# Matmul operands and weight loads: where the buffers start modulo 512 bytes

## The chip, the cores and the metric

One core of a Trainium2 chip runs the whole kernel as one program. The metric is the device time of that program in microseconds, the median of several runs. All buffers that are spoken of here lie in the on-chip memory (SBUF), which has 128 partitions; a buffer starts at the same byte in each of them. TensorE runs each matmul as two instructions: a weight load, which puts the stationary operand (128x128 numbers, 512 bytes in each partition) into the array, and the matmul, which streams the moving operand (256 or 512 numbers, 1024 or 2048 bytes in each partition) through it. The profile shows them as PEld and PE.

## The reference

The reference is one layer of a decoder trunk for 256 tokens of width 2048, all in float32: adaLN modulation from a condition vector, four token mixers on one input projection, an output projection, and a gated feed-forward net of width 5632.

```python
mod = (silu(c) @ w_mod + b_mod)              # sh1, sc1, g1, sh2, sc2, g2
h = rmsnorm(x, norm_mix) * (1 + sc1) + sh1
proj = h @ w_in                              # 2048 x 5660, for all four mixers
y = concat([gla(...), gated_deltanet(...), pool(...), forgetting_attention(...)]) @ w_out
x = x + g1 * y
h = rmsnorm(x, norm_ffn) * (1 + sc2) + sh2
gate = causal_dwconv(h @ w_gate, conv_w) + conv_b
x = x + g2 * ((silu(gate) * (h @ w_up)) @ w_down)
out = rmsnorm(x, norm_final)
```

## The kernel before

Every large product is made of three matmuls on numbers that are split in two: a high part (a cast to float32r, by ScalarE) and a low part (the difference, by VectorE). `split` (L113 to L116) does it; its two instructions are the groups L115 ACT CAST and L100 DVE TENSOR_TENSOR. The product is high x high + high x low + low x high.

Weights are streamed in blocks of 128x1024 numbers. `load` (L155) brings one into `wr` (five buffers, in turn), `load_split` makes `wh` and `wl` of it (three buffers each, in turn). The activations stand in one large buffer, `bigA`: high and low parts of the normalised input (`HL`), then of the mixers' outputs (`Y2`), then of the second normalised input (`H2`), each 2048 bytes to a block `k` of 128 features: 256 tokens of high part, 256 of low part. All matmuls go through the helper `mm` (L97), so that the profile tells them apart by their tiles alone: out<-moving,stationary.

The stages in order of time:

- Input projection (`ext` and `acc` as outputs, from about 60 to 478 us, in the second half between the mixers' own small products `gdt`, `oxt` and the condition's products `bgt`). `gdn` and `pair` run, for each block and each 128 outputs, three matmuls of 256 columns: `wh` as stationary with the high and the low activations moving, then `wl` with the high ones. Some pairs (`tok`) have it the other way round: activations stationary, `wh`, `wl`, `wh` moving.
- Output projection (`project`, `wot`, to 547 us): activations stationary, `wh`, `wl`, `wh` moving; 512 columns wide, in the last two of five chunks 256.
- Feed-forward, gate and up (`proj`, outputs `fpt` from `bigA`, about 553 to 1046 us): 22 calls of `proj` with 16 blocks `k` each. For a block: four weight loads of `wh`, each with one matmul of 512 columns (the high and the low activations side by side), and four of `wl`, each with one matmul of 256 columns (the high ones). This document calls such a block, eight matmuls, a step; there are 352.
- Feed-forward, down (`fpt` from `AH`, `AL`, 1046 to 1289 us): stationary is `AH` (high part of the gated activations) twice, then `AL` (low part); moving is `wh`, `wl`, `wh`, always 512 wide. 1056 matmuls.

The weight load of the next matmul runs while a matmul runs. So while a matmul of gate and up reads `bigA`, the load reads `wh` or `wl`; while one of down reads `wh` or `wl`, the load reads `AH` or `AL`. The document names such a pair by its distance: start of what the load reads minus start of what the matmul reads, modulo 512 bytes. All blocks within a buffer are multiples of 512 bytes, so that one number holds for a whole buffer.

Where the buffers lie follows from the order and the size of the tiles in the pools `keep` (first) and `wp` (second), then the pools of the phases. In the built program:

| buffer | start, before | mod 512 | start, after | mod 512 |
|---|---|---|---|---|
| `bigA` | 19808 | 352 | 19360 | 416 |
| `wr` (first) | 73120 | 416 | 72608 | 416 |
| `wh` (first) | 93600 | 416 | 93088 | 416 |
| `wl` (first) | 105888 | 416 | 105440 | 480 |
| `AH` | 134560 | 416 | 134560 | 416 |
| `AL` | 179616 | 416 | 179680 | 480 |

Of the kernel before, what the change touches and what calls it, by code (L numbers as in the profile page):

```python
# [8 lines left out]
F32 = mybir.dt.float32  # L9
F32R = mybir.dt.float32r  # L10
# [6 lines left out]
P = 128  # L17
D = 2048
KT = D // P
T = 256  # L20
NT = T // P
FF = 5632
NF = FF // P
# [23 lines left out]
NG = len(GROUPS)  # L47

TAKE = (16, 12, 11)

ORDER = "gpfd"

# [21 lines left out]
def trunk_kernel(ctx: ExitStack, tc: tile.TileContext, x, c, w_mod, b_mod, norm_mix, norm_ffn, w_in,  # L74
# [3 lines left out]
    nc = tc.nc  # L78
# [12 lines left out]
    wp = ctx.enter_context(tc.tile_pool(name="wp", bufs=3))  # L91

    def kt_(shape, name, dt=F32):
        return keep.tile(shape, dt, name=name, tag=name)

    def mm(o, l, r, start=True, stop=True):
        PE.matmul(o, lhsT=l, rhs=r, start=start, stop=stop, skip_group_check=True)  # L97

    def tt(o, a, b, op):
        V.tensor_tensor(out=o, in0=a, in1=b, op=op)  # L100
# [13 lines left out]
    def split(hi, lo, src):  # L114
        S_.copy(hi, src)  # L115
        tt(lo, src, hi.bitcast(F32), ALU.subtract)  # L116
# [4 lines left out]

    ident = kt_([P, P], "ident")
    nc.sync.dma_start(ident, cst[:, K_ID:K_ID + P])
    crow = kt_([KT, P], "crow")
    nc.sync.dma_start(crow, c[0].rearrange("(k p) -> k p", p=P))
    ones = kt_([P, P], "ones")
    V.memset(ones, 1.0)

# [12 lines left out]
    s2 = kt_([P, KT], "s2")  # L141
    sh2 = kt_([P, KT], "sh2")

    bigA = lambda: keep.tile([P, KT, 2 * T], F32R, name="bigA", tag="bigA")
    bigC = lambda: keep.tile([P, KT * T], F32, name="bigC", tag="bigC")

# [6 lines left out]
    def load(view, k0, nk, c0, n):  # L153
        wr = wp.tile([P, 1024], F32, name="wr", tag="wr", bufs=5).rearrange("p (k n) -> p k n", n=n)
        nc.sync.dma_start(wr[:, 0:nk], view[:, k0:k0 + nk, c0:c0 + n])  # L155
        return wr

    def load_split(view, k0, nk, c0, n):
        wr = load(view, k0, nk, c0, n)
        wh = wp.tile([P, 1024], F32R, name="wh", tag="wh", bufs=3).rearrange("p (k n) -> p k n", n=n)  # L160
        wl = wp.tile([P, 1024], F32R, name="wl", tag="wl", bufs=3).rearrange("p (k n) -> p k n", n=n)
        split(wh[:, 0:nk], wl[:, 0:nk], wr[:, 0:nk])
        return wh, wl

# [63 lines left out]
    with ExitStack() as ph:  # L228
# [59 lines left out]
        with ExitStack() as st:  # L288
            sp = st.enter_context(tc.tile_pool(name="sp", bufs=1, reuse_waits="tile"))
            acp = st.enter_context(tc.tile_pool(name="acp", bufs=1, space=PSUM, reuse_waits="tile"))  # L290
            xt = sp.tile([P, NT, D], F32, name="xt")
            r1 = sp.tile([P, P], F32, name="r1")
            r2 = sp.tile([54, P], F32, name="r2")
            r3 = sp.tile([2 * NF, P], F32, name="r3")
# [115 lines left out]
            def gdn(g):  # L410
                k0, nk = GROUPS[g]
                for k2 in range(k0, k0 + nk, 2):
                    for c3 in range(3):
                        wh, wl = load_split(wi_v, k2, 2, C_QKV + 512 * c3, 512)
                        for kk in range(2):
                            k = k2 + kk
                            for f in range(4):
                                ft = c3 * 4 + f
                                o = acc[ft // 2][:, ft % 2]
                                fs = slice(f * P, f * P + P)  # L420
                                mm(o, wh[:, kk, fs], HL[:, k, 0:T], start=False, stop=False)
                                mm(o, wh[:, kk, fs], HL[:, k, T:], start=False, stop=False)
                                mm(o, wl[:, kk, fs], HL[:, k, 0:T], start=False, stop=k == KT - 1)
                        yield
# [13 lines left out]
            def pair(p, g0, g1):  # L438
                c0, tok, dst, scale = pairs[p]
                k0, k1 = GROUPS[g0][0], sum(GROUPS[g1 - 1])  # L440
                a = ext().rearrange("p (f t) -> p f t", t=T)
                for ka in range(k0, k1, 4):
                    kb = min(ka + 4, k1)
                    wh, wl = load_split(wi_v, ka, kb - ka, c0, 256)
                    for f in range(2):
                        for k in range(ka, kb):
                            fs = slice(f * P, f * P + P)
                            first, last = f == 0 and k == k0, k == k1 - 1
                            if tok:
                                xh, xl = HL[:, k, fs], HL[:, k, T + f * P:T + f * P + P]  # L450
                                three = ((xh, wh[:, k - ka]), (xh, wl[:, k - ka]), (xl, wh[:, k - ka]))
                            else:
                                xh, xl = HL[:, k, 0:T], HL[:, k, T:]
                                three = ((wh[:, k - ka, fs], xh), (wh[:, k - ka, fs], xl), (wl[:, k - ka, fs], xh))
                            for i, (l, r_) in enumerate(three):
                                mm(a[:, f], l, r_, start=first and i == 0, stop=last and i == 2)
                    yield
                with tc.high_priority():
                    add(dst, a, g0 == 0, scale)
# [10 lines left out]
            def extras(g):  # L470
                ps = range(len(pairs) - TAKE[g], len(pairs)) if g < NG - 1 else range(len(pairs))
                for p in ps:
                    yield from pair(p, done[p], g + 1)
                    done[p] = g + 1
# [472 lines left out]
        chunks = ((0, 512), (512, 512), (1024, 512), (1536, 256), (1792, 256))  # L947
        Y2 = bigA()

        def project(n, a):  # L950
            c0, w = chunks[n]
            nk = 1024 // w
            for j in range(KT // nk):
                ks = order[nk * j:nk * j + nk]
                if n == 0:
                    for k in ks:
                        split(Y2[:, k, 0:T], Y2[:, k, T:], pr[:, k + 4])
                wh, wl = load_split(wo_v, ks[0], nk, c0, w)
                steps = [(kk, k, t) for kk, k in enumerate(ks) for t in range(NT)]
                if n == len(chunks) - 1 and ks[-1] == order[-1]:  # L960

                    steps.sort(key=lambda s: s[2])
                for kk, k, t in steps:
                    st, sp_ = j + kk == 0, nk * j + kk == KT - 1
                    xh, xl = Y2[:, k, t * P:t * P + P], Y2[:, k, T + t * P:T + t * P + P]
                    mm(a[t], xh, wh[:, kk], start=st, stop=False)
                    mm(a[t], xh, wl[:, kk], start=False, stop=False)
                    mm(a[t], xl, wh[:, kk], start=False, stop=sp_)
# [5 lines left out]
        x1 = bigC().rearrange("p (t d) -> p t d", t=NT)  # L974
        for t in range(NT):
            nc.sync.dma_start(x1[:, t], x_v[:, t])
        x1s = kt_([P, NT, len(chunks)], "x1s")
        with tc.tile_pool(name="op", bufs=2, reuse_waits="tile") as op:
            for n, (c0, w) in enumerate(chunks):
                ns, gs = slice(c0, c0 + w), slice(c0 % 1024, c0 % 1024 + w)  # L980
# [11 lines left out]
    with ExitStack() as ph:  # L992
# [27 lines left out]
                stt(H2[:, k, T:], h, sh2[:, k:k + 1], H2[:, k, 0:T].bitcast(F32), ALU.add, ALU.subtract)  # L1020

        ap_ = ph.enter_context(tc.tile_pool(name="ap", bufs=1, reuse_waits="tile"))
        AH = ap_.tile([P, NF, T], F32R, name="AH")
        AL = ap_.tile([P, NF, T], F32R, name="AL")

        def proj(gp, view, c0):
# [17 lines left out]
        with tc.tile_pool(name="gp", bufs=2, reuse_waits="tile") as gp:  # L1044
            for n in range(NF // 4):
                gt = proj(gp, wg_v, 512 * n)
                ut = proj(gp, wu_v, 512 * n)
                for i in range(4):
                    f = 4 * n + i
# [6 lines left out]
                    tt(cv, ut[i], cv, ALU.mult)  # L1056
                    split(AH[:, f], AL[:, f], cv)

# [3 lines left out]
        with tc.tile_pool(name="op2", bufs=1, reuse_waits="tile") as op:  # L1062
            chunks = ((0, 512), (512, 512), (1024, 512), (1536, 512))
            fs = op.tile([P, NT, len(chunks) + 1], F32, name="fs")
            f1 = op.tile([P, 4], F32, name="f1")
            for n, (c0, w) in enumerate(chunks):
# [6 lines left out]
                for g in range(NF // nk):  # L1073
                    wh, wl = load_split(wd_v, nk * g, nk, c0, w)
# [5 lines left out]
                    for k, t, h_, l_ in steps:  # L1080
                        ts = slice(t * P, t * P + P)
                        mm(a[t], AH[:, k, ts], h_, start=k == 0, stop=False)
                        mm(a[t], AH[:, k, ts], l_, start=False, stop=False)
                        mm(a[t], AL[:, k, ts], h_, start=False, stop=k == NF - 1)
# [58 lines left out]
```

## Time and profile before

| | us |
|---|---|
| median of three runs | 1299.4 |
| lowest, highest | 1298.0, 1302.43 |
| the profiled execution | 1305.52 |
| its span, first to last instruction | 1303.7 |
| TensorE busy in the span | 1247.2 (96%) |
| VectorE, ScalarE busy | 888.9 (68%), 636.6 (49%) |
| mean granted TensorE clock | 0.981 |

The rows of a group read: line, engine, operation, out<-moving,stationary, shape, count, then busy time in us, mean duration of one in ns, and the engine's idle time before them. The end of a matmul is modelled and matmuls overlap, so that a duration is longer than the step from one start to the next; a matmul's own slowness shows in both.

### The profile page before, as it was taken

Reading aid. Unit: us, or ns where it says so; the run is one execution under the profiler, and the core shown is the slowest. Engines: PE = TensorE matmul, PEld = TensorE weight load, DVE = VectorE, ACT = ScalarE, POOL = GpSimd, SP = SyncE. Lnnn points to the kernel's source line nnn. Section 1 sums busy time; section 2 is a strip of 40 time slices with the busy share of each in tenths; the row PEclk is TensorE's granted clock in tenths of the full one; section 3 lists DMA queues with packets and bytes.
Section 4 is the critical chain, followed back from the end, with each engine's and each line's share of the span. In section 5 each row is a group of like instructions: output and inputs, shape, how many; then the busy total and the mean of one; then the engine's idle time right before and its main releaser. Section 6 shows DMA issues by size and latency. Waiting matters only on the chain.

```text
span 1303.7 us, 19845 instructions
## 1 busy us (share of the span) xinstructions
PE 1247.2 (96%) x7663; PEld 1078.8 (83%) x7663; DVE 888.9 (68%) x1201; ACT 636.6 (49%) x1000; POOL 23.5 (2%) x31
## 2 busy tenths in 40 slices
PE   2799999999999999999999999999999999999995
PEld 1699999898976687888888888888888888888884
DVE  7578797989763387676666656665756687974543
ACT  3455344674364454555555545554555553443432
POOL 0200000010000000000000000000000000000000
PEclk8799999999999999999999999999999999999998
DMA  9999998796557888656666666657666699875662
GB/s 329 270 367 377 320 335 295 250 336 224 174 200 255 311 315 286 176 148 190 180 196 192 180 197 190 190 165 211 190 184 175 208 353 381 306 258 188 194 193 82
DMA packets 168597, 311.91 MB, mean 239 GB/s; under 512 B 16172, under 2 KB 54067, under 8 KB 167863
## 3 DMA queue, kind: packets, MB, share of 16 engines
q1 hardware_dynamic: 168503, 310.65, 72.9%
q8 instruction: 60, 0.98, 0.3%
q14 instruction: 34, 0.28, 0.1%
HBM read 308.51 MB, written 2.10 MB: 238 GB/s over the span
## 4 chain that ended last, share of the span: by engine, by line
PE 91%; DMA 4%; DVE 1%; SPq 1%; ACT 1%; issue 1%; POOLq 0%; ACTq 0%; DVEq 0%
PE fpt L97 56%; PE ext L97 16%; PE wot L97 5%; PE gdt L97 4%; PE acc L97 4%; DMA wm<-in_w_mod_dram 4%; PE bgt L97 3%; PE oxt L97 2%; DMA wr<-in_w_in_dram 1%; DVE ga L103 1%; ACT xT L1011 0%; DVE m L100 0%; DVE wl L100 0%; SPq L399 0%; PE oxt L873 0%
## 5 line engine op out<-in xcount | busy, mean ns | idle before, releaser
L100 DVE TENSOR_TENSOR wl<-wr,wh 128x1024 fp32r<-128x1024 f32 x384 | 469.0, 1222 | 296.8 <-ACT wh L115 296.1
L115 ACT CAST wh<-wr 128x1024 fp32r<-128x1024 f32 x384 | 403.5, 1051 | 490.2 <-PE fpt L97 314.9
L97 PE MATMUL fpt<-bigA,wh 128*128 128x512 f32 x1408 | 399.3, 395 | 2.1 <-DVE bigA L103 2.1
L97 PEld LDWEIGHTS fpt<-bigA,wh 128*128 128x128 f32 x1408 | 239.0, 188 | 32.8 <-issue 2.2
L97 PEld LDWEIGHTS fpt<-bigA,wl 128*128 128x128 f32 x1408 | 222.8, 189 | 34.5 <-DVE wl L100 3.7
L97 PE MATMUL fpt<-bigA,wl 128*128 128x256 f32 x1408 | 240.7, 279 | 0.0
L103 DVE SCALAR_TENSOR_TENSOR ga<-wm,cond,ga 128x1024 f32<-128x1024 f32 x139 | 177.9, 1280 | 14.1 <-DMA wm<-in_w_mod_dram 13.2
L97 PE MATMUL ext<-bigA,wh 128*128 128x256 f32 x768 | 138.4, 282 | 0.0
L97 PE MATMUL fpt<-wl,AH 128*128 128x512 f32 x352 | 137.5, 391 | 0.0
L97 PE MATMUL fpt<-wh,AL 128*128 128x512 f32 x352 | 137.0, 389 | 0.0
L97 PE MATMUL fpt<-wh,AH 128*128 128x512 f32 x352 | 123.4, 390 | 0.0
L97 PEld LDWEIGHTS ext<-bigA,wh 128*128 128x128 f32 x768 | 118.5, 190 | 3.1 <-DVE E L100 0.8
L97 PE MATMUL ext<-bigA,wl 128*128 128x256 f32 x384 | 107.9, 281 | 1.7 <-DVE wl L100 1.7
L97 PEld LDWEIGHTS fpt<-wl,AH 128*128 128x128 f32 x352 | 66.1, 188 | 14.3 <-DVE wl L100 0.4
L97 PEld LDWEIGHTS fpt<-wh,AH 128*128 128x128 f32 x352 | 66.1, 188 | 14.1 <-ACT wh L115 0.2
L97 PEld LDWEIGHTS fpt<-wh,AL 128*128 128x128 f32 x352 | 66.1, 188 | 14.0 <-issue 0.2
L97 PEld LDWEIGHTS ext<-bigA,wl 128*128 128x128 f32 x384 | 72.9, 190 | 2.9 <-DVE wl L100 1.9
L97 PE MATMUL acc<-bigA,wh 128*128 128x256 f32 x384 | 68.7, 285 | 5.6 <-ACT bigA L115 3.2
L97 PE MATMUL ext<-wh,bigA 128*128 128x256 f32 (+1 forms) x320 | 69.3, 308 | 0.0
L97 PEld LDWEIGHTS acc<-bigA,wh 128*128 128x128 f32 x384 | 59.7, 195 | 6.0 <-ACT bigA L115 3.3
L97 PE MATMUL wot<-wh,bigA 128*128 128x512 f32 (+1 forms) x256 | 63.0, 337 | 0.0
L97 PEld LDWEIGHTS ext<-wh,bigA 128*128 128x128 f32 x320 | 52.9, 192 | 5.5 <-issue 1.4
(340 smaller groups left out, 1193.2 us busy)
## 6 DMA issues: line engine op xcount, KB each, us to landing
wm<-in_w_mod_dram SPq DMA_DIRECT2D x192, 512.0 KB, 5.6
wr<-in_w_in_dram SPq DMA_DIRECT2D x88, 512.0 KB, 9.1
wr<-in_ffn_w_gate_dram SPq DMA_DIRECT2D x88, 512.0 KB, 3.7
wr<-in_ffn_w_up_dram SPq DMA_DIRECT2D x88, 512.0 KB, 4.3
wr<-in_ffn_w_down_dram SPq DMA_DIRECT2D x88, 512.0 KB, 4.6
wr<-in_w_out_dram SPq DMA_DIRECT2D x32, 512.0 KB, 4.2
xt<-in_x_dram SPq DMA_DIRECT2D x2, 1024.0 KB, 7.1
bigC<-in_x_dram SPq DMA_DIRECT2D x2, 1024.0 KB, 9.1
```

The lines of the kernel that those rows point to most:

```text
L97: PE.matmul(o, lhsT=l, rhs=r, start=start, stop=stop, skip_group_check=True)
L100: V.tensor_tensor(out=o, in0=a, in1=b, op=op)
L103: V.scalar_tensor_tensor(out=o, in0=a, scalar=s, in1=b, op0=op0, op1=op1)
L115: S_.copy(hi, src)
```

## The change

Three things move the buffers. `x1s` (a small tile of sums) and `crow` (the condition vector as rows) change pools, so that `bigA` starts 64 bytes later modulo 512. The three buffers of `wh` become three tiles of their own, and the third is 64 bytes longer, so that `wl` starts 64 bytes beyond `wh` modulo 512. In the feed-forward phase a filler tile ahead of `AH` and 64 bytes behind it put `AH` at the same place as `bigA` and `wh`, and `AL` 64 bytes beyond.

```diff
+LINE = 64
...
-    crow = kt_([KT, P], "crow")
-    nc.sync.dma_start(crow, c[0].rearrange("(k p) -> k p", p=P))
...
+    x1s = kt_([P, NT, 5], "x1s")
...
+    loads, whs = [0], []
+
     def load_split(view, k0, nk, c0, n):
         wr = load(view, k0, nk, c0, n)
-        wh = wp.tile([P, 1024], F32R, name="wh", tag="wh", bufs=3).rearrange("p (k n) -> p k n", n=n)
+        i = loads[0] % 3
+        loads[0] += 1
+        if loads[0] == 1:
+            for j in range(3):
+                whs.append(wp.tile([P, 1024], F32R, name=f"wh{j}", tag=f"wh{j}", bufs=1,
+                                   padded_shape=[P, 1024 + LINE // 4 * (j // 2)]))
+            wh = whs[0]
+        else:
+            wh = wp.tile([P, 1024], F32R, name=f"wh{i}", tag=f"wh{i}", bufs=1) if loads[0] > 3 else whs[i]
         wl = wp.tile([P, 1024], F32R, name="wl", tag="wl", bufs=3).rearrange("p (k n) -> p k n", n=n)
+        wh = wh.rearrange("p (k n) -> p k n", n=n)
...
+            crow = sp.tile([KT, P], F32, name="crow")
+            nc.sync.dma_start(crow, c[0].rearrange("(k p) -> k p", p=P))
...
-        x1s = kt_([P, NT, len(chunks)], "x1s")
...
-        AH = ap_.tile([P, NF, T], F32R, name="AH")
+        ap_.tile([P, (512 - LINE) // 4], F32, name="gap")
+        AH = ap_.tile([P, NF * T], F32R, name="AH", padded_shape=[P, NF * T + LINE // 4]).rearrange("p (f t) -> p f t", t=T)
```

The built program has the same instructions in the same order on every engine and queue as before, but for one separate wait of ScalarE ahead of the first copy into `AH`, which is gone. What changes otherwise is addresses alone. The distances, by stage:

| stage, matmul running -> next load | distance before | after |
|---|---|---|
| gate/up, 512 wide -> `wh` (three of four) | 64 | 0 |
| gate/up, 512 wide -> `wl` (the fourth) | 64 | 64 |
| gate/up, 256 wide -> `wl` (three of four) | 64 | 64 |
| gate/up, 256 wide -> `wh` (the fourth) | 64 | 0 |
| down, all | 0 | 0 |
| `gdn`, `pair`: next load `wh` (two of three) | 64 | 0 |
| `gdn`, `pair`: next load `wl` (one of three) | 64 | 64 |
| `project`, `tok`: `wh` moving (two of three) | 448 | 0 |
| `project`, `tok`: `wl` moving (one of three) | 448 | 448 |

## The prediction

> **What bounds the kernel now.** I read the page first, its busy times and its chain that ended last, to see which engine a change must shorten.
>
> ```profile
> PE 1247.2 (96%) x7663; PEld 1078.8 (83%) x7663; DVE 888.9 (68%) x1201; ACT 636.6 (49%) x1000; POOL 23.5 (2%) x31
> ...
> PE 91%; DMA 4%; DVE 1%; SPq 1%; ACT 1%; issue 1%; POOLq 0%; ACTq 0%; DVEq 0%
> ```
>
> TensorE holds 91% of the chain. The chain in order of time has one piece that covers the whole feed-forward net, with no other engine in it:
>
> ```profile
> 553.49 734.96 PE fpt L97 x3875
> ```
>
> So 735 us, more than half of the span, end when the matmuls end, and a nanosecond on each of them comes out at the end. The view by stretches says how full the two halves are (columns: length, PE, PEld, DVE, ACT, POOL busy, granted clock, DMA share, GB/s):
>
> ```profile
> 553.50:1046.10 492.60, 492.60 (x2816) 427.55 (x2817) 311.89 (x452) 261.41 (x399) 0.00 (x0) 1.00 0.63 186
> 1046.20:1289.00 242.80, 242.80 (x1065) 199.24 (x1064) 159.11 (x154) 100.53 (x114) 0.95 (x1) 1.00 0.71 251
> ```
>
> Clock 1.00 in both, VectorE at 312 of 493 us, DMA at 0.63: nothing but the matmuls' own pace. That pace is the thing to look at, and two views give it. First the groups, shapes kept apart, gate/up in the first two rows, down in the other three:
>
> ```profile
> L97 PE MATMUL fpt<-bigA,wh 128*128 128x512 f32 x1408 | 399.3, 395 | 2.1 <-DVE bigA L103 2.1
> L97 PE MATMUL fpt<-bigA,wl 128*128 128x256 f32 x1408 | 240.7, 279 | 0.0
> L97 PE MATMUL fpt<-wl,AH 128*128 128x512 f32 x352 | 137.5, 391 | 0.0
> L97 PE MATMUL fpt<-wh,AL 128*128 128x512 f32 x352 | 137.0, 389 | 0.0
> L97 PE MATMUL fpt<-wh,AH 128*128 128x512 f32 x352 | 123.4, 390 | 0.0
> ```
>
> The same instruction, 128x512 with a 128x128 weight load beside it, lasts 395 ns on average in gate/up (distance 64) and 389 to 391 in down (distance 0). Then the order of time, ten steps of gate/up and ten matmuls of down; the first column is the start:
>
> ```profile
> 700.25 1.09 PE L97 MATMUL fpt<-bigA,wh 128*128 128x512 f32 x4
> 701.17 0.62 PE L97 MATMUL fpt<-bigA,wl 128*128 128x256 f32 x4
> ...
> 714.11 1.09 PE L97 MATMUL fpt<-bigA,wh 128*128 128x512 f32 x4
> 715.04 0.62 PE L97 MATMUL fpt<-bigA,wl 128*128 128x256 f32 x4
> ```
>
> ```profile
> 1150.05 0.39 PE L97 MATMUL fpt<-wh,AL 128*128 128x512 f32 x1
> ...
> 1152.31 0.39 PE L97 MATMUL fpt<-wh,AL 128*128 128x512 f32 x1
> ```
>
> Ten steps take 714.11 - 700.25 = 13.86 us, 1386 ns each. In down ten matmuls start between the two rows (nine rows, the first of the two among them, and one of the nine holds two) in 2.26 us, 226 ns each. At down's pace four matmuls of 512 take 904 ns; in gate/up they take 920 to 930.
>
> Where in the step the excess sits is seen by asking for stretches so short that one matmul alone runs in them. The four of 512 in one step (from 802.06 us), in order, then the four of 256, two at a time:
>
> ```profile
> L97 PE MATMUL fpt<-bigA,wh 128*128 128x512 f32 x1 | 0.4, 388 | 0.0
> L97 PE MATMUL fpt<-bigA,wh 128*128 128x512 f32 x1 | 0.4, 398 | 0.0
> L97 PE MATMUL fpt<-bigA,wh 128*128 128x512 f32 x1 | 0.4, 393 | 0.0
> L97 PE MATMUL fpt<-bigA,wh 128*128 128x512 f32 x1 | 0.4, 398 | 0.0
> L97 PE MATMUL fpt<-bigA,wl 128*128 128x256 f32 x2 | 0.4, 278 | 0.0
> L97 PE MATMUL fpt<-bigA,wl 128*128 128x256 f32 x2 | 0.4, 276 | 0.0
> ```
>
> The excess comes in pieces of 5 ns: none, two, one, two; then one on the first of 256 (a mean of 278 for two), none on the rest. Something is lost in whole pieces while a matmul and a load read at once at distance 64, and in down, at distance 0, hardly anything.
>
> **The change, part by part.** It issues the same instructions in the same order. What costs or gains is what each pair of readers does at its new distance.
>
> *Gate/up, the first three matmuls of 512 of each step: 64 to 0.* Nearest row: down, the same shapes at distance 0. 388 + 398 + 393 = 1179 ns become three of 389 or 390: 9 to 12 ns a step, times 352 steps = 3.2 to 4.2 us. All on the path. I take 3.8.
>
> *Gate/up, the fourth of 512 (the next load is `wl`): stays at 64.* It lasts 398 now. It may stay (0), or, following three undisturbed ones, behave like the first of a step now does (388): 10 ns x 352 = 3.5 us. I take 0.5, near the lower end, since its own distance is not changed and its row says 398.
>
> *Gate/up, 256 wide.* The first has one piece (5 ns, 1.8 us over 352), the others next to none; the group's mean of 279 against 276 for an undisturbed one bounds it all: 3 ns x 1408 = 4.2 us. The first follows the fourth of 512, whose fate it probably shares; the last gets distance 0. No row shows 256 wide at distance 0, so a loss stands open too, bounded by one piece on that last one: 5 x 352 = 1.8 us. I take a gain of 0.5 between -1.8 and +4.2.
>
> *Down: 0 before, 0 after,* since `AL` moves along with `wl` and `AH` stays with `wh`. Nothing, both ways.
>
> *Input projection, 256 wide.* One undisturbed stretch, the four main groups:
>
> ```profile
> L97 PE MATMUL ext<-bigA,wh 128*128 128x256 f32 x160 | 27.7, 278 | 0.0
> L97 PE MATMUL acc<-bigA,wh 128*128 128x256 f32 x138 | 23.3, 278 | 0.0
> L97 PE MATMUL ext<-bigA,wl 128*128 128x256 f32 x80 | 22.3, 278 | 1.7 <-DVE wl L100 1.7
> L97 PE MATMUL acc<-bigA,wl 128*128 128x256 f32 x67 | 17.5, 278 | 0.0
> ```
>
> Their counts in the whole run (the means here hold waits too):
>
> ```profile
> L97 PE MATMUL ext<-bigA,wh 128*128 128x256 f32 x768 | 138.4, 282 | 0.0
> L97 PE MATMUL ext<-bigA,wl 128*128 128x256 f32 x384 | 107.9, 281 | 1.7 <-DVE wl L100 1.7
> L97 PE MATMUL acc<-bigA,wh 128*128 128x256 f32 x384 | 68.7, 285 | 5.6 <-ACT bigA L115 3.2 <-ACT wh L115 2.4
> L97 PE MATMUL acc<-bigA,wl 128*128 128x256 f32 x192 | 52.2, 284 | 0.8 <-DVE wl L100 0.8
> ```
>
> 2 ns above 276, on 768 + 384 + 384 + 192 = 1728 matmuls: 3.5 us if every pair became clean; two of three go to distance 0: 2.3 us. The other bound is a loss: a piece of 5 ns instead of 2 on those two thirds, 1152 x 3 = 3.5 us. Not all would reach the end, since before 257 us a wait for weights ends on DMA, not on TensorE:
>
> ```profile
> 249.34 7.75 DMA wm<-in_w_mod_dram
> ```
>
> What is won ahead of it is waited away there as long as that transfer does not come sooner. I take 1.0.
>
> *Output projection.*
>
> ```profile
> L97 PE MATMUL wot<-wh,bigA 128*128 128x512 f32 x128 | 40.4, 394 | 0.0
> L97 PE MATMUL wot<-wh,bigA 128*128 128x256 f32 x128 | 22.8, 279 | 0.0
> ```
>
> 394 against 390 on `wh` at 448, of which there are 128 and in the first chunk 64 more: 192 x 4 = 0.8 us; 279 against 276: 128 x 3 = 0.4 us. The pairs that stay at 448 gain nothing. I take 0.8 of 0 to 1.2 (the products before 257 us that have activations as weights are within the rounding of this).
>
> *`crow`, `x1s`, filler, the lost wait.* `crow`'s transfer is at the same place in SP's queue. `split` now writes `wl` 64 bytes off from `wr` and `wh`; should VectorE slow down by it, its 312 busy us in the 492.6 of gate/up leave room for half as much again. ScalarE's lost wait stood once, beside TensorE's work. Nothing.
>
> *Sum.* 3.8 + 0.5 + 0.5 + 1.0 + 0.8 = 6.6 us off. The profiled execution took 1305.5 (span 1303.7 and 1.8 around it) and would take 1298.9; it is 6.1 above the median of the three runs, which lies in no step of the sum, so I take it off the median: 1299.4 - 6.6 = 1292.8.
>
> **A rule that speaks against it.** The Trainium skill, "TensorE: Matmul & The Clock Gate", Part 2 (Step-by-step), says that TensorE has two independent read ports and that loading the next weights takes no read bandwidth from the running matmul; "SBUF — State Buffer" (Who interferes with whom) adds "PE and ACT never wait on anyone". By this rule no address changes a pace, and the sum would be 0. The rows above stand against it, 388 to 398 ns for one instruction at full clock with nothing else different in the step, but they do not prove that addresses are the cause.
>
> **The rivals.**
>
> 1. *Distance is not the cause; the time stays.* What is lost may come of alternating widths (512, then 256) or of PSUM, since gate/up has both widths and down one. For it: within one step at one and the same distance the loss is 0, 10, 5, 10. Against it: `wot` at 512 alone, no widths alternating, has 394 at distance 448, where down has 390. Time: 1299.4. This is also what the rule of the skill gives.
>
> 2. *In line is worse where widths alternate; slower.* At distance 0 both readers start at the same place modulo 512 at nearly the same time. If in gate/up each of 512 then lost two pieces (398) and each of 256 one (281, that is 278 x 2 - 276 = 280 by the row), it would cost 1408 x (398 - 394) + 1408 x (280 - 277) = 5.6 + 4.2 = 9.8 us: 1309. It decides from 1.4 ns per matmul on (3.9 us over 2816). Against it: down's 1056 matmuls at distance 0, at 389 to 391, show no piece.
>
> 3. *All of the loss goes, also where the distance stays 64.* If the pieces are handed on from one matmul to the next (the first of a step is clean at 64), one clean matmul makes the next clean. Then a step takes 4 x 226 + 4 x 113 = 1356 to 1360 ns instead of 1386: 26 to 30 ns x 352 = 9 to 10.5 us, with 3 us from the projections some 13: 1286.5. For it: the history in the step. Against: the fourth of 512 has its own distance.
>
> **How the numbers follow.** A measurement of this kernel tells about 0.3%, 3.9 us, from no change. The forecast (4 to 10 us off, 1289.5 to 1295.5) has 0.58; rival 3 (beyond 10 us) 0.10; rival 1, or gains too small to tell, 0.22; rival 2 or any loss beyond 0.3% 0.10. So faster 0.68, same 0.22, slower 0.10. The range runs from rival 3's time, 1286.5, to just above no change, 1300, and leaves out rival 2 and the tails. Predicted: 1292.8.
>
> **What would show it.** In the profile after: `fpt<-bigA,wh` at 391 to 393 on average instead of 395; in one step 389, 389, 389 and then, in question, 398 or 388 on the fourth; ten steps in 13.70 to 13.75 us (13.6 by rival 3); down unchanged at 389 to 391 and 226 ns a matmul; the piece of chain `fpt` some 5 us shorter than 734.96; `wot` at 512 near 391. The prediction is wrong if the step still takes 1386 ns (rival 1), if the three in line show 393 or 398 (rival 2), or if gate/up gains and the projections lose as much because 256 wide at distance 0 is worse than at 64.

## The result and the profile after

The changed kernel takes 1311.78 us (median of 4 runs, 1310.86 to 1313.0) against 1299.62 for the kernel before beside it: ratio 1.0085, 95% interval [1.0071, 1.01], some 11 us slower by the ratio, 12 by the medians. The forecast was 1292.8, faster than before.

The page after, groups with shapes kept apart, the same five as before (a helper's line is now L99 instead of L97):

```profile
L99 PE MATMUL fpt<-bigA,wh 128*128 128x512 f32 x1408 | 398.8, 395 | 2.1 <-DVE bigA L105 2.1
L99 PE MATMUL fpt<-bigA,wl 128*128 128x256 f32 x1408 | 244.6, 282 | 0.0
L99 PE MATMUL fpt<-wl,AH 128*128 128x512 f32 x352 | 138.4, 393 | 0.0
L99 PE MATMUL fpt<-wh,AL 128*128 128x512 f32 x352 | 138.2, 392 | 0.0
L99 PE MATMUL fpt<-wh,AH 128*128 128x512 f32 x352 | 125.1, 395 | 0.0
```

The first row is what was to go from 395 to 392: it stands still. The second went from 279 to 282. And down, whose own distances were 0 and stayed 0, went from 391, 389 and 390 to 393, 392 and 395. The chain's piece of the feed-forward net says the same in one number, 742.24 for 734.96 us:

```profile
553.11 742.24 PE fpt L99 x3875
```

It is split by stretches. The first stretch is gate/up, 3.6 us longer than the 492.6 of before, at the same full clock and with the same number of matmuls; the rest of the 7.3 us is down:

```profile
553.20:1049.40 496.20, 496.20 (x2816) 432.73 (x2817) 311.86 (x452) 261.58 (x399) 0.00 (x0) 1.00 0.62 185
```

In order of time, ten steps of gate/up, and ten matmuls of down:

```profile
700.83 1.09 PE L99 MATMUL fpt<-bigA,wh 128*128 128x512 f32 x4
701.75 0.64 PE L99 MATMUL fpt<-bigA,wl 128*128 128x256 f32 x4
...
714.83 1.09 PE L99 MATMUL fpt<-bigA,wh 128*128 128x512 f32 x4
715.75 0.52 PE L99 MATMUL fpt<-bigA,wl 128*128 128x256 f32 x3
```

```profile
1160.19 0.40 PE L99 MATMUL fpt<-wh,AL 128*128 128x512 f32 x1
...
1162.50 0.39 PE L99 MATMUL fpt<-wh,AL 128*128 128x512 f32 x1
```

A step takes 14.00 us / 10 = 1400 ns (1386 before): 920 ns for the four of 512, as before, and 480 for the four of 256, about 15 more. Down takes 231 ns a matmul (226 before). The four of 512 in one step, each from a stretch that holds it alone:

```profile
L99 PE MATMUL fpt<-bigA,wh 128*128 128x512 f32 x1 | 0.4, 396 | 0.0
L99 PE MATMUL fpt<-bigA,wh 128*128 128x512 f32 x1 | 0.4, 397 | 0.0
L99 PE MATMUL fpt<-bigA,wh 128*128 128x512 f32 x1 | 0.4, 389 | 0.0
L99 PE MATMUL fpt<-bigA,wh 128*128 128x512 f32 x1 | 0.4, 392 | 0.0
```

So distance 0 does not give 389 at once: the first two of a step, just after four of 256, are slow, the third is clean. In the input projection (the same stretch as before, 120 to 180 us) 278 has become 282:

```profile
L99 PE MATMUL ext<-bigA,wh 128*128 128x256 f32 x160 | 28.5, 282 | 0.0
L99 PE MATMUL ext<-bigA,wl 128*128 128x256 f32 x80 | 22.7, 283 | 1.7 <-DVE wl L102 1.7
L99 PE MATMUL acc<-bigA,wh 128*128 128x256 f32 x129 | 22.3, 282 | 0.0
```

4 ns on the 1728 matmuls of that kind would be 7 us. From start to start, over the whole input projection, the two traces have 114.9 and 117.9 ns on average for such a matmul where none waits, which makes about 5 us. The single profile of before does not show them in its total, since it happened to reach the output projection late: its first `wot` piece starts at 478.34 us, that of the changed kernel at 477.41, those of later kernels with the old places in the input projection between 471.63 and 477.21.

### The profile page after: what moved, and what is told of

It reads as the page before. It is cut to its first block, busy times and chain, and to the rows that moved or that the text cites. A ratio compares the mean times of both kernels' runs of the same rounds, so it can differ in the third digit from the quotient of the medians.

```text
span 1310.6 us, 19844 instructions
## 1 busy us (share of the span) xinstructions
PE 1257.0 (96%) x7663; PEld 1086.6 (83%) x7663; DVE 889.4 (68%) x1201; ACT 635.7 (49%) x1000; POOL 22.7 (2%) x31
## 4 chain that ended last, share of the span: by engine, by line
PE 91%; DMA 5%; DVE 1%; SPq 1%; ACT 1%; issue 1%; POOLq 0%; ACTq 0%; DVEq 0%
PE fpt L99 57%; PE ext L99 16%; PE wot L99 5%; PE gdt L99 4%; PE bgt L99 3%; PE acc L99 3%; DMA wm<-in_w_mod_dram 3%; PE oxt L99 2%; DMA wr<-in_w_in_dram 1%; DVE ga L105 1%; DMA ct<-in_cst_dram 0%; ACT xT L1024 0%; ACT wh L117 0%; DVE wl L102 0%; DVE m L102 0%
## 5 line engine op out<-in xcount | busy, mean ns | idle before, releaser
L117 ACT CAST wh<-wr 128x1024 fp32r<-128x1024 f32 x384 | 403.1, 1050 | 497.6 <-PE fpt L99 320.7
L99 PE MATMUL fpt<-bigA,wh 128*128 128x512 f32 x1408 | 398.8, 395 | 2.1 <-DVE bigA L105 2.1
L99 PEld LDWEIGHTS fpt<-bigA,wh 128*128 128x128 f32 x1408 | 242.4, 190 | 33.2 <-issue 2.2
L99 PEld LDWEIGHTS fpt<-bigA,wl 128*128 128x128 f32 x1408 | 223.9, 188 | 32.5 <-DVE wl L102 4.0
L99 PE MATMUL fpt<-bigA,wl 128*128 128x256 f32 x1408 | 244.6, 282 | 0.0
L99 PE MATMUL ext<-bigA,wh 128*128 128x256 f32 x768 | 139.9, 283 | 0.0
L99 PE MATMUL fpt<-wl,AH 128*128 128x512 f32 x352 | 138.4, 393 | 0.0
L99 PE MATMUL fpt<-wh,AL 128*128 128x512 f32 x352 | 138.2, 392 | 0.0
L99 PE MATMUL fpt<-wh,AH 128*128 128x512 f32 x352 | 125.1, 395 | 0.0
L99 PEld LDWEIGHTS ext<-bigA,wh 128*128 128x128 f32 x768 | 118.0, 188 | 3.0 <-issue 1.2
L99 PE MATMUL ext<-bigA,wl 128*128 128x256 f32 x384 | 108.6, 283 | 1.7 <-DVE wl L102 1.7
L99 PEld LDWEIGHTS fpt<-wl,AH 128*128 128x128 f32 x352 | 66.1, 188 | 15.4 <-DVE m L102 0.2
L99 PEld LDWEIGHTS fpt<-wh,AL 128*128 128x128 f32 x352 | 66.1, 188 | 15.4 <-issue 0.2
L99 PEld LDWEIGHTS fpt<-wh,AH 128*128 128x128 f32 x352 | 66.2, 188 | 15.0 <-ACT wh L117 0.2
L99 PEld LDWEIGHTS ext<-bigA,wl 128*128 128x128 f32 x384 | 73.5, 192 | 2.8 <-DVE wl L102 1.9
L99 PE MATMUL acc<-bigA,wh 128*128 128x256 f32 x384 | 70.7, 289 | 3.7 <-ACT bigA L117 2.6
L99 PE MATMUL ext<-wh,bigA 128*128 128x256 f32 (+1 forms) x320 | 69.9, 310 | 0.0
L99 PEld LDWEIGHTS acc<-bigA,wh 128*128 128x128 f32 x384 | 60.3, 196 | 4.1 <-ACT bigA L117 2.7
L99 PE MATMUL wot<-wh,bigA 128*128 128x512 f32 (+1 forms) x256 | 63.4, 338 | 0.0
L99 PEld LDWEIGHTS ext<-wh,bigA 128*128 128x128 f32 x320 | 53.1, 193 | 5.7 <-issue 1.4
```

## The experiments

Three accounts of the loss: *distance* (as forecast: a pair at 0 is clean, anything else pays), *mixture* (loads and matmuls that follow each other at different places modulo 512 disturb each other), *place* (480 itself is bad). Each kernel is timed against the kernel before on the same chip. The diffs are shortened; "..." and words in brackets stand for code.

### All in line, at three places, and AL alone

```diff
# all416: the kernel before, x1s ahead of bigA
+    x1s = kt_([P, NT, 5], "x1s")
     bigA = lambda: keep.tile(...)
# all480, all0: and a filler of 64 or 96 bytes there
+    kt_([P, 64 // 4], "fill")
# al480: the kernel before, AH 64 bytes longer
-        AH = ap_.tile([P, NF, T], F32R, name="AH")
+        AH = ap_.tile([P, NF * T], F32R, name="AH", padded_shape=[P, NF * T + 16]).rearrange(...)
```

All at 416:

> The kernel before with x1s ahead of bigA, so that bigA, wh, wl, AH and AL all start at 416 modulo 512: every distance is 0. By mixture (what costs is that loads or matmuls that follow each other start at different places modulo 512) and by distance alone, every matmul goes at the pace that down had before: 128x512 at 226 to 227 ns from start to start, a gate/up step of 1356 to 1365 ns, time 1285 to 1291 us. By place (480 itself is bad) the same. If width (512 and 256 in turn) is what costs in gate/up, the step stays at 1386 ns and the time at 1299.

All at 480:

> As the kernel with all at 416, and a filler of 64 bytes ahead, so that all five buffers start at 480. By mixture and by distance alone: the same time as with all at 416, within 2 us. By place: slower than that, each 128x512 at 229 to 233 ns in down as in the changed kernel, 1300 to 1312 us.

All at 0:

> As the kernel with all at 416, with a filler of 96 bytes, so that all five buffers start at 0 modulo 512 (and at a multiple of 64, where all kernels so far start at 32 modulo 64). By mixture and by distance alone: the same time as with all at 416, within 2 us. By place, with the 64-byte grid as what counts: faster than all the others, the 128x512 pace below 226 ns.

AL alone at 480:

> The kernel before with AL alone 64 bytes further (480), nothing else moved; gate/up stays as it was, 1386 ns a step. By mixture, down slows from 226-227 to 229 ns or more for each 128x512, some 3 to 5 us, time 1302 to 1305. By distance alone, only the matmuls ahead of a load of AL (one of three, now 64) slow, by up to 10 ns: 0 to 3.5 us, and the other two keep 226-227. By place: only those whose load reads AL slow.

Measured: 1313.1 us, ratio 1.0095 [1.0072, 1.0118]; 1312.85, 1.0091 [1.0064, 1.0117]; 1309.08, 1.0065 [1.0042, 1.0088]; 1305.05, 1.0034 [1.0019, 1.0049].

All three accounts had forecast 1285 to 1291 us for all at 416, and all three missed; so did a fourth, that alternating widths cost by themselves and the time stays (1299). Place falls: for 416, 480 and 0 (a multiple of 64) the intervals overlap, and the matmul groups of gate/up and down agree within 1 ns. Distance alone and mixture alone fall too, since with everything in line neither leaves anything to lose. The groups of the kernel with all at 416:

```profile
L97 PE MATMUL fpt<-bigA,wh 128*128 128x512 f32 x1408 | 400.2, 396 | 2.1 <-DVE bigA L103 2.1
L97 PE MATMUL fpt<-bigA,wl 128*128 128x256 f32 x1408 | 244.6, 282 | 0.0
L97 PE MATMUL fpt<-wl,AH 128*128 128x512 f32 x352 | 137.5, 390 | 0.0
```

and, from 120 to 180 us, its input projection:

```profile
L97 PE MATMUL ext<-bigA,wh 128*128 128x256 f32 x160 | 29.0, 283 | 0.0
L97 PE MATMUL acc<-bigA,wh 128*128 128x256 f32 x125 | 21.9, 283 | 0.0
L97 PE MATMUL ext<-wh,bigA 128*128 128x256 f32 x32 | 5.9, 283 | 0.0
```

At distance 0, 512 wide in a long run is clean (down, 390), and 256 wide in a long run is slow: 283, 7 ns above 276. In line is good for one width and bad for the other. Gate/up, with both widths at distance 0, gets neither.

What stands of mixture is weaker: a neighbour's place counts, and AL alone shows it. Its three groups of down:

```profile
L97 PE MATMUL fpt<-wh,AL 128*128 128x512 f32 x352 | 138.5, 394 | 0.0
L97 PE MATMUL fpt<-wl,AH 128*128 128x512 f32 x352 | 138.2, 393 | 0.0
L97 PE MATMUL fpt<-wh,AH 128*128 128x512 f32 x352 | 124.7, 394 | 0.0
```

Only the matmuls ahead of a load of `AL` (one in three) have another distance than before. All three kinds slow down, by 2 to 5 ns (389, 391 and 390 before): what one pair loses is handed on to the next.

### The changed kernel without bigA's move, and a sweep of distances

```diff
# wl_al480: the changed kernel, but x1s stays where it was (bigA at 352)
# d128, d256, d384 (and below d320, d96): the kernel before, crow moved as in the change, filler behind bigA
         x1s = kt_([P, NT, len(chunks)], "x1s")
+        kt_([P, FILL // 4], "fill")      # FILL = 64, 192, 320 (256, 32)
```

wl and AL at 480:

> The changed kernel without its first part: bigA stays at 352 (wh, wr, AH at 416), wl and AL at 480 as in the changed kernel. Down is then placed as in the changed kernel. By mixture: down at 229 to 233 ns a matmul, 3.5 to 4 us more than before; gate/up has wh at distance 64 as before and wl at 128, and where it slows too (from 1386 to 1395 ns or more a step) mixture explains it without the move of bigA; time 1303 to 1310. If mixture costs in down alone, gate/up stays at 1386 and the time is 1303 to 1305, and the rest of the changed kernel's 12 us is bigA's move.

Distance 128:

> One filler behind bigA: bigA at 352; wh, wl, AH and AL all at 480, so that the distance is 128 in the input projection and gate/up, 0 in down, 384 in the output projection. If load and matmul meet once at any distance but 0 (the matmul reads 512 bytes twice as fast as the load does), 128 costs about what 64 does: 256 wide at 113 to 118 ns, 512 wide at 226 to 236, time 1297 to 1302. If 64 is a lucky place, slower: 1303 to 1312. Down at 226-227 either way.

Distance 256:

> As the one with 128, the distance 256 (and 256 in the output projection too). If they meet once at any distance but 0: 1297 to 1302, 256 wide at 113 to 118. If 64 is a lucky place: 1303 to 1312. If far apart is best (4 pieces of 64 bytes between them): 1285 to 1294.

Distance 384:

> As the one with 128, the distance 384 in the input projection and gate/up, 128 in the output projection. If they meet once at any distance but 0: 1297 to 1302. If 64 is a lucky place: 1303 to 1312. The output projection had 384 with the first of these fillers: its 512 wide matmuls tell whether only the distance counts or also which of the two buffers is read by the load.

Measured: 1310.52, ratio 1.0063 [1.0046, 1.008]; 1310.88, 1.0065 [1.0047, 1.0083]; 1311.97, 1.0074 [1.0052, 1.0095]; 1311.96, 1.0068 [1.0043, 1.0092].

Moving `wl` and `AL` off alone costs most of it: gate/up goes to 1400 ns a step with `bigA` where it was,

```profile
700.00 1.09 PE L97 MATMUL fpt<-bigA,wh 128*128 128x512 f32 x4
...
714.00 1.09 PE L97 MATMUL fpt<-bigA,wh 128*128 128x512 f32 x4
```

and its groups of down are at 393, 392 and 395, as in the changed kernel. Either part alone (`bigA`'s move in the kernel with all at 416, the other here) loses about as much as both together. And "once at any distance but 0" falls, since 128, 256 and 384 all lose. What shows is a period. With 256 the input projection (120 to 180 us) reads like that of distance 0 above,

```profile
L97 PE MATMUL ext<-bigA,wh 128*128 128x256 f32 x160 | 29.0, 283 | 0.0
...
L97 PE MATMUL ext<-wh,bigA 128*128 128x256 f32 x32 | 5.9, 283 | 0.0
```

and 128 and 384 agree with each other (gate/up 395 and 281 in both). In the means of gate/up all four are within 1 ns, so the order inside a step is what tells them apart: the four of 512 take 234, 235, 232 and 228 ns from start to start at 0 and at 256 alike, and 233, 232, 236 and 231 at 128 and at 384 alike. The output projection stands at 384 when gate/up stands at 128, and the other way round. Its 512 wide groups are 397 and 403 in both, so there it does not matter which of the two buffers the load reads.

### The period, a place between, and fewer changes of width

```diff
# group0 (on all416), group64 (on the kernel before): in proj
-                for kk in range(2):
-                    (four of 512 with wh[kk], four of 256 with wl[kk])
+                for kk in range(2):
+                    (four of 512 with wh[kk])
+                for kk in range(2):
+                    (four of 256 with wl[kk])
```

Distance 320:

> As the one with 128, the distance 320. The traces of 0 and 256 agree with each other, and those of 128 and 384 too, as if the distance counted modulo 256. By that, 320 is the same as 64, the kernel before: gate/up step 1386 ns, 256 wide in the input projection at 113 to 114 for more than half, time 1297 to 1302. If the period is 512 after all and 64 is a lucky place, 1308 to 1313, as with 128, 256 and 384.

Eight and eight at distance 0:

> The kernel with all five buffers at 416 (distance 0), and in gate/up the eight 512 wide matmuls of a block of weights ahead of its eight 256 wide ones (before: four and four). If it is the change of width that takes gate/up off down's pace, half of the changes give back about half of the loss at 512: the later ones of the eight at 226-227, mean below 231 (232.7 with four and four), gate/up 3 us shorter or more, while 256 wide stays at 118 to 120. If the loss at 512 belongs to gate/up for another reason, the mean stays at 232 to 233 and the time at 1312.

Eight and eight at distance 64:

> The same order, eight and eight, with the buffers where the kernel before has them (distance 64 in gate/up). Before, the four of 512 take 226, 236, 231, 236 and the four of 256 118, 114, 114, 114. If the loss is handed on within a run of one width, the later ones of 512 stay at 231 to 236 (gate/up up to 1 us longer, since the clean first one is rarer) and the later ones of 256 at 113-114 (1 us shorter): the same time within 2 us. If runs settle at a clean pace, 5 us shorter.

Distance 96:

> As the one with 128, the distance 96, a place between 64 (256 wide at 115 on average) and 128 (118.7). If the price goes evenly with the distance: 256 wide at 116 to 118, time 1303 to 1308. If what counts is that buffers stand at odd multiples of 32 apart, no longer aligned to each other by 64, it can be anything from 1290 to 1315; no row speaks for either.

Measured: 1300.24, ratio 0.9991 [0.9976, 1.0006]; 1309.36, 1.0067 [1.0044, 1.0091]; 1299.31, 0.9983 [0.9968, 0.9998]; 1314.02, 1.0097 [1.0071, 1.0123].

320 is the kernel before again, to 0.1% in time and in the chain, where 742 stood for the changed kernel:

```profile
549.69 734.93 PE fpt L97 x3875
```

So in all three pairs that were tried (0 and 256, 128 and 384, 64 and 320) the distance counts modulo 256 bytes. With 96 gate/up takes 500.5 us, more than with 64 (492.7) and 128 (496.3), so the price does not go evenly between them.

Eight and eight at distance 0 (order of time, one run of each width):

```profile
701.97 2.00 PE L97 MATMUL fpt<-bigA,wh 128*128 128x512 f32 x8
703.81 1.11 PE L97 MATMUL fpt<-bigA,wl 128*128 128x256 f32 x8
704.76 2.00 PE L97 MATMUL fpt<-bigA,wh 128*128 128x512 f32 x8
```

1840 ns for eight of 512, 230 each (four and four: 232.7 on average from start to start), and 119 for each of 256. Gate/up, from its first matmul to down's first, takes 493.4 us instead of the 497.6 of the kernel with all at 416: the change of width is what takes the 512s off down's pace, while the 256s stay slow. After five matmuls of a run of eight the 512s are at 227 ns. At distance 64 the same order gives 233 and 114, and 488.2 us instead of 492.7; the kernel keeps about half of it (ratio 0.9983), and its down takes 244.7 us instead of 243.0:

```profile
703.23 2.02 PE L97 MATMUL fpt<-bigA,wh 128*128 128x512 f32 x8
705.09 1.07 PE L97 MATMUL fpt<-bigA,wl 128*128 128x256 f32 x8
706.00 2.02 PE L97 MATMUL fpt<-bigA,wh 128*128 128x512 f32 x8
```

### What was still open: the changed kernel's own pair of distances

```diff
# after_group8: the changed kernel with the eight-and-eight order
# stage8, stage16: bigA 64 bytes longer, HL at its start, Y2 and H2 64 bytes in;
#   wl buffers 256 bytes longer, read 64 bytes in by gate/up, at the start by all others
+    def bigA(off=0): ...        # Y2 = bigA(16), H2 = bigA(16)
+    def load_split(view, k0, nk, c0, n, off=0): ...   # gate/up: off = 16
# stage16 and control16: two weight blocks at a time in proj, sixteen of 512, then sixteen of 256
# control16: those longer buffers and that order, every offset 0 (places as in the kernel before)
```

The changed kernel, eight and eight:

> The changed kernel, buffers as in it, with gate/up's eight matmuls of 512 of a weight block ahead of its eight of 256. In the changed kernel gate/up has 512 wide at distance 0 and 256 wide at distance 64, each the best place that the runs showed for a long run of one width (226.7 and 113.3), but four and four. If the changes between the two are what spoils it: gate/up goes from 496.2 us to below that of the kernel before (492.6), 484 to 491, and the time falls by 5 to 12 us against the changed kernel, to 1300 to 1307; down and the projections keep their loss. If the two places do not go together at all: no gain, 1311.

Places by stage, eight and eight:

> The best place for each stage, by offsets into buffers that are a little longer: input projection at distance 64 as before, output projection at 0, gate/up 512 wide at 0 and 256 wide at 64, eight and eight, down all at 0. By width, distance and changes of place: input projection as before, output projection 0.5 us less, gate/up 484 to 491 us, down as before at 243; time 1292 to 1299. If places that change from stage to stage or buffer to buffer cost by themselves: 1300 or more.

Places by stage, sixteen and sixteen:

> As the one before, with two weight blocks at a time in gate/up: sixteen matmuls of 512, then sixteen of 256. If each run of one width settles within some six matmuls, twice as long runs halve what is lost to settling: gate/up 479 to 487 us, time 1288 to 1295, unless the casts of two blocks at a time make TensorE wait (three buffers each for wh and wl), which would show as idle time ahead of wl.

Old places, sixteen and sixteen:

> The order of the one before (sixteen and sixteen) and its longer buffers, but every place as in the kernel before (distance 64 in gate/up, 448 in the output projection). It tells order from place: by place, gate/up stays at 490 to 494 us and the time at 1297 to 1302; if the order alone is what gains, it is as fast as the one with sixteen and the chosen places.

Measured: 1307.11, ratio 1.0039 [1.0026, 1.0052]; 1298.8, 0.9973 [0.9961, 0.9985]; 1297.34, 0.9959 [0.9943, 0.9975]; 1296.52, 0.9957 [0.9945, 0.9969].

One buffer of `wl` in three stands 256 bytes off the other two in the last three kernels, modulo 512, and `AH` and `AL` stand 256 off `wh`; by the period that is the same place, and down keeps its old 391, 389 and 390 within 1 ns there.

With half the changes of width the changed kernel's gate/up takes 491.5 us, 4.8 less than with four and four and 1.2 less than before, just short of what was expected, and the ratio falls from 1.0085 to 1.0039. Most of the gain is the 512s' (229.7 ns from start to start on average for 231.7); the 256s stay at 118, though 113 had been the best seen at their distance. So the two distances go together only in part. What remains is down (394, 392 and 395, the changed kernel's within 1 ns) and the projections. Places by stage, with eight and eight, bring down back to its old pace and leave gate/up at 491.4 us, again just short of what was expected. Sixteen and sixteen with the same two distances shows what each width does when left alone:

```profile
700.22 3.81 PE L97 MATMUL fpt<-bigA,wh 128*128 128x512 f32 x16
703.87 2.05 PE L97 MATMUL fpt<-bigA,wl 128*128 128x256 f32 x16
705.76 3.81 PE L97 MATMUL fpt<-bigA,wh 128*128 128x512 f32 x16
```

Sixteen of 512 at distance 0: 3.65 us, 228 each; they do settle, at 227 from the sixth on. Sixteen of 256 at distance 64: 1.89 us, 118 each. The control, both at 64:

```profile
701.48 1.98 PE L97 MATMUL fpt<-bigA,wl 128*128 128x256 f32 x16
703.29 3.89 PE L97 MATMUL fpt<-bigA,wh 128*128 128x512 f32 x16
707.02 1.98 PE L97 MATMUL fpt<-bigA,wl 128*128 128x256 f32 x16
```

233 for 512 (231 and 236 in turn, start to start), and 1.81 us, 113 each, for 256. The same 256 wide matmuls, at the same distance of 64, run at 113 after a run of 512 at 64 and at 118 after a run of 512 at 0, for all sixteen of them. So a distance has more than one steady pace, and in gate/up of these two kernels it goes with the run ahead. The 80 ns lost on sixteen of 256 eat up the 80 ns won on sixteen of 512, and so places by stage and old places come out alike (0.9959 and 0.9957, gate/up 490.6 and 490.0 us); the 479 to 487 us expected of the chosen places were missed for this reason. In the changed kernel, four and four, the 512s do not even get as far as settling, and the 256s pay all the same.

The 256s go with the run ahead of them in most runs, not in all. Of the 77 runs of sixteen 256s that each of the two traces holds whole, 74 go at 118 with the chosen places and 66 at 113 in the control; the others go at the other pace. And in the input projection neither places nor order settle it. Up to the output projection the kernel with `AL` alone moved has the same matmuls in the same order at the same addresses as the kernel before. From 118 to 132 us, first the kernel before, then the other, both at full clock:

```profile
L97 PE MATMUL acc<-bigA,wh 128*128 128x256 f32 x84 | 14.1, 276 | 0.0
L97 PE MATMUL acc<-bigA,wh 128*128 128x256 f32 x80 | 13.9, 281 | 0.0
```

276 is a step of 113 here, and 281 one of 118. In these two traces and in those with sixteen and sixteen, a pace lasts for up to 358 matmuls on end and never changes inside an unbroken row of such matmuls; it changes only where a wait or other matmuls come between. What picks it there is open.

The last three beat both kernels of this study. Gate/up gives the control 2.7 of its 5.6 us, by order alone; the rest lies ahead of the output projection, which kernels with the same distances there reach at different times (471.63 to 478.34 us). The two paces account for little of that (118 instead of 113 on 35% of the 256s in the kernel before and on 17% in the control, some 1.3 us), and the rest is not explained.

## Why the prediction was wrong

- *TensorE's own pace sets the end; nothing else moved.* Right: the loss is in the matmuls' pace at full clock, with the same instructions in the same order. Rival 1 (no effect) is refuted: places alone moved the time by some 11 us. The Trainium skill, "TensorE: Matmul & The Clock Gate", Part 2 (Step-by-step), says that a weight load takes no read bandwidth from the running matmul. Here the same 256 wide matmul takes 113 or 118 ns at one set of places and 120 at another, and the measurement decides; whether it is read bandwidth that is lost, no run shows.
- *Gate/up, the first three of 512 at down's pace: 3.8 us off.* This is the step that failed first. It took down's 389 to 390, measured in a run of 1056 matmuls of one width and one place, for the price of distance 0 as such. Just after 256s the first two take 396 and 397, and the three together 1182 ns, where 1179 were to become 1167 to 1170. On average the 512s are where they were (395): nothing won.
- *Gate/up, the fourth of 512: a gain of 0.5 between 0 and 3.5.* In sign right: 398 became 392 at an unchanged distance, some 2 us. But the first of a step, put down as one of the three to be won, went from 388 to 396 and took that back.
- *Gate/up, 256 wide: a gain of 0.5 between -1.8 and +4.2.* Mis-sized, and outside its bounds: 279 became 282, 3 ns x 1408 = 4.2 us lost. The bound for a loss allowed one piece on the one matmul in four whose distance changed. From start to start (medians of the stage) the four went from 118, 113, 113, 113 to 118, 118, 117, 121: the last, now at distance 0, lost 8, and the second and third, at an unchanged 64, lost 4 to 5 each. What changed for those two is the run of 512s ahead of them; that this is the reason fits the experiments, but is not isolated.
- *Down: nothing, both ways.* Wrong by 3.7 us. Each pair kept its distance, but one of two neighbours moved, and AL alone repeats it (393, 394, 394).
- *Input projection: a gain of 1.0 between -3.5 and +2.3.* Wrong in sign: 278 became 282. The 278 was misread, too: it is no loss of 2 ns on every matmul but a mean of two paces, 276 from 118 to 132 us and 281 from 160 to 180. All at 0 gave 283, so two pairs of three went to a slow place for 256 wide. The loss bound (a piece of 5 instead of 2 on two thirds) was near it for those two thirds; the last third lost too.
- *Output projection: 0.8 off.* Wrong: `wh` at 512 wide went to distance 0 and from 394 to 397 ns (row below, of the changed kernel's groups), with `wl` left at 448 in between; with all at 416 it is at 393. The stage as a whole took 68.9 us for 68.3, so this loss is small.

```profile
L99 PE MATMUL wot<-wh,bigA 128*128 128x512 f32 x128 | 40.8, 397 | 0.0
```

- *The rivals.* Rival 2 had the sign and the size (9.8 us, 1309) and the right words, in line is worse where widths alternate; but it put the whole price into gate/up, which lost 3.6, and had neither down nor the input projection, so that its size came out by luck. Its argument against, that down shows no piece at distance 0, was the same mistake as in the sum.

Gate/up (3.6) and down (3.7) are 7.3 us of the 11 to 12; the rest is put down to the projections, where 3 to 4 ns on 1728 narrow matmuls are 5 to 7 us less what the waits for weights take up. That part is an estimate: the two profiled executions, 1305.52 and 1312.42 us, do not show it as a difference ahead of the output projection.

The flaw behind all of them: the paces of before were read as a function of the pair's distance alone, although the quoted step (388, 398, 393, 398 at one distance) showed that they are not. That row was counted for rivals 1 and 3, and not against the sum.

## What to carry to other kernels

A pace that is measured in one long, even run of matmuls holds for that run: before it is carried to a stage that mixes widths or buffers, look whether equal pairs in that stage have equal times at all. Where weight loads hide under matmuls, moving buffers by 64 bytes can cost a per cent (0.3 to 1.0% here, and no move of buffers alone gained), and a neighbour that moves can cost as much as the pair itself; so a layout is tried, stage by stage, and not reasoned out. Keeping matmuls of one width together took 2.7 to 4.5 us off gate/up with no distance changed, and made the kernel 0.2 to 0.4% faster, in part for reasons that are not explained.

## What the hardware showed that was not expected

- The pace of a matmul depends on where the weight load beside it and its neighbours read, modulo 256 bytes in the three pairs tried: 0 and 256 agree (256 wide at 283 ns in the input projection), 128 and 384 agree (281 in gate/up), 320 equals 64 (ratio 0.9991).
- In long runs, distance 0 is clean for 512 wide (226 to 227 ns from start to start) and costs 6 to 7 ns on 256 wide (119 to 120 for 113); at distance 64 it is 233 for 512 and 113 or 118 for 256.
- One distance has several steady paces, 113 and 118 ns for 256 wide at 64, kept for up to 358 matmuls on end. In gate/up the pace goes with the run ahead in most runs; in the input projection the same matmuls at the same places took either in different executions. How the two reads meet inside the memory was not shown; only that the loss comes in pieces of about 5 ns in the kernel before and is handed on.
